# The gates of the banded branch as two column pairs instead of one pair and two single blocks

## The chip, the cores and the metric

The kernel runs on one core of one Trainium2 chip. The metric is the device time of one execution in microseconds (us), as the median of several runs. The profile names the core's engines so: PE is TensorE (matmuls), PEld its weight loads, DVE is VectorE, ACT is ScalarE, POOL is GpSimd and SP is SyncE. SP and POOL here mostly issue DMA transfers.

## The reference

One decoder layer on 256 tokens of width 2048, all in float32. The part that matters here:

```
P  = rms_norm(x) @ W_in            # columns: MLA latents, band q/k/v, gates gA and gB (2048 each)
A  = dense latent attention (16 heads)
Bq = banded attention (32 query heads, 4 kv heads, window 128)
y  = W_out( sigmoid(gA) * (A @ Wo_A) + sigmoid(gB) * (Bq @ Wo_B) )
x  = x + rms_norm(y)
x  = x + rms_norm(conv_ffn(rms_norm(x)))
```

The banded branch's share of the sum is sigmoid(gB) * (Bq @ Wo_B). gB and Bq @ Wo_B are each a product of 256 x 2048 with 2048 x 2048, worked in four blocks of 512 columns.

## The kernel before, in words

**Precision.** Each float32 operand is split into a high part, in the reduced format that TensorE multiplies (`fp32r`), and a low part, the rest. A product is three matmuls: high by high, high by low, low by high (`mm3`, lines 198 to 201). A matmul takes 128 rows of the contraction, 128 tokens and 512 columns.

**Weights.** They stream from HBM in chunks of 128 x 1024 numbers (512 KB). `convert` (lines 153 to 166) lets ACT write the high part `whi` and DVE subtract it to get the low part `wlo`. These go to rings of four slots (`RING`), so an engine can only run four conversions ahead of PE. SP issues the loads into a ring of raw buffers.

**The plain block.** `gemm` (line 203) works 512 columns for both token tiles: 16 row tiles, two to a chunk, 96 matmuls, eight chunks. After each chunk it calls `tick`, which runs the steps that `at(t, f)` has put down for that count of ticks. The program's order is made in this way; a scheduler then orders each engine's queue by readiness and by that order. A queue runs strictly in its order on the chip.

**The pair.** `pair_gemm` (line 274) works 1024 columns, as two halves, for both token tiles, in the manner of Strassen and Winograd: two row tiles, two token tiles and two column halves make a 2 x 2 by 2 x 2 product. Its order string has a letter for each two row tiles. A `p` is a plain unit, two chunks of 12 matmuls each. An `s` is a unit of seven products instead of eight (21 matmuls). Its weights are loaded by POOL's queue (lines 325 to 327) to a place `gr`. DVE makes four sums of them (`weight_sums`, lines 229 to 234), each 128 x 512, into `gta` and `gtb`. Then one conversion each of the odd row tile, half of the even one, `gta` and `gtb`, two ticks in all. For its token side `token_sums` (line 376) makes sums of four 128 x 128 blocks, once for each unit. The pair has four accumulators `c` in one half of PSUM and four `q` in the other; at the end `end_sums` (line 350) adds the `q` into the four tiles `d` and `finish_gate` (line 829) adds `c` and takes the tanh.

**PSUM.** There are eight banks: `pacc` has four, `pss` and `pst` two each. A plain block takes two, from `pacc` unless it is told otherwise; a pair takes all eight, the `q` banks from its first seven-product unit on. `pst` also serves transposes.

**Order around the change.** The last block of latents (line 769, 320 columns) leaves two `pacc` banks that ACT reads (lines 774, 733, 734). Two small transposes of its result (`krT`, `ckT`, lines 779 to 788) follow three and six ticks into the next product. Then come:

1. gate block 0, plain (`gate_b`, line 795);
2. output block 0, Bq @ Wo_B (`out_b`, line 804), with accumulators in `pss`; the token sums of the pair are put down here (line 839);
3. gate blocks 1 and 2 as a pair, order `psppspsp`;
4. output block 1 in `pss`; gate block 3, plain; output block 2 in `pacc`. Over these three run four `park_a` steps (line 843), one in five ticks. Each loads 1 MB of the weights of the last layer part into a buffer `gr`, makes four sums of them on DVE and stores the results in HBM for later (`park_sums`, line 238). There are two `gr` buffers, which the pair's loads use too.

Then comes the dense latent attention, with output block 3 (line 1001) under it. `out_b` ends each block with DVE's product of gate and accumulator (line 807) and a store by POOL's queue (line 808). The gate tiles come from a pool `stg` of four slots.

Of the kernel before, what the change touches and what calls it, by code (L numbers as in the profile page):

```python
# [15 lines left out]
AF = mybir.ActivationFunctionType  # L16
# [3 lines left out]
P = 128  # L20
D = 2048
S = 256
NT = 2
KT = D // P
# [12 lines left out]
C_GB = 5440  # L37
# [5 lines left out]
def trunk_layer(ctx, tc, x, x_cols_in, conv_cols_in, g_mix_post, g_ffn_post, w_in, w_q, w_kv,  # L43
                sinks, rel, wo_a, wo_b, w_out, w_up, w_down, rope_tab, strip_sel, out):
    nc = tc.nc
    vec, act, pe, pool = nc.vector, nc.scalar, nc.tensor, nc.gpsimd
# [7 lines left out]
    pss = ctx.enter_context(tc.tile_pool(name="pss", bufs=2, space=PS))  # L54
# [5 lines left out]
    def sb(pl, shape, name, dt=F32, tag=None, bufs=None):  # L60
        return pl.tile(shape, dt, name=name, tag=tag or name, **({"bufs": bufs} if bufs else {}))
# [41 lines left out]
    cnt = [0]  # L103
# [75 lines left out]
    now = [0]  # L179

    def at(t, *fs):
        steps[max(t, now[0])].extend(fs)
# [10 lines left out]
    def new_acc(tag, ps=None):  # L193
        i = cnt[0]
        pl, pt = ps or (pacc, "acc")
        return [pl.tile([P, 512], F32, name=f"acc{tag}_{i}_{t}", tag=pt) for t in range(NT)]

    def mm3(o, ah, al, bh, bl, start, stop):
        pe.matmul(o, ah, bh, start=start, stop=False)  # L199
        pe.matmul(o, ah, bl, start=False, stop=False)  # L200
        pe.matmul(o, al, bh, start=False, stop=stop)  # L201

    def gemm(xh, xl, w, k0, nk, c0, n, split=None, extra=None, ps=None):

        kc = 1024 // n if n in (256, 512) else 2
        acc = new_acc("g", ps)
        todo = []
        cuts = list(range(0, nk, kc)) + [nk]
        for ci, (k, ke) in enumerate(zip(cuts[:-1], cuts[1:])):
            kk = ke - k  # L210
            src = w[(k0 + k) * P:(k0 + k + kk) * P, c0:c0 + n].rearrange("(a p) n -> p a n", p=P)
            hi, lo = wchunk(src, [kk, n], *(extra or {}).get(ci, ()))
            for j in range(kk):
                kt = k + j
                wh, wl = hi[:, j * n:(j + 1) * n], lo[:, j * n:(j + 1) * n]
                for t in range(NT):
                    x_ = [x(k0 + kt)[:, t * P:(t + 1) * P] for x in (xh, xl)]
                    if split is None or t == 0 or ci < split:
                        mm3(acc[t][:, :n], *x_, wh, wl, kt == 0, kt == (split * kc if split and t else nk) - 1)
                    else:  # L220
                        todo.append((kt, x_, wh, wl))
            tick()
        return acc, todo
# [46 lines left out]
    def park_a(i, pl, tag, t0, **kw):  # L270
        u, p = (i, 0) if i < NA[0] else (i - NA[0], 1)
        return park_sums(f"ta{i}_", w_down, 2 * u, 1024 * p, pl, tag, t0, **kw)
# [186 lines left out]
    XH, XL = pair_view(highs(xt)), pair_view(lows(xt))  # L459
# [6 lines left out]
    rh = sb(base, [P, NT], "rh")  # L466
# [246 lines left out]
    for g in range(4):  # L713
        acc = gemm(XH, XL, w_in, 0, KT, C_QS + 512 * g, 512)[0] if g else acc_q0
# [12 lines left out]
    stg = lambda name, n=512: sb(lpool, [P, n], name, tag="stg", bufs=STG)  # L727
# [36 lines left out]
    acc, _ = gemm(XH, XL, w_in, 0, KT, 0, 512)  # L764
# [4 lines left out]
    acc, _ = gemm(XH, XL, w_in, 0, KT, C_KV, KVR + ROPE)  # L769
# [22 lines left out]
    yb_d = dram.tile([4, NT, P, 512], F32, name="yb_d")  # L792
    x2_d = dram.tile([NT, P, D], F32, name="x2_d")

    def gate_b(j):
        acc, _ = gemm(XH, XL, w_in, 0, KT, C_GB + 512 * j, 512)
        tb = []
        for t in range(NT):
            g = stg(f"tb{j}_{t}")
            act.activation(g, acc[t], AF.Tanh, scale=rh[:, t:t + 1])  # L800
            tb.append(g)
        return tb

    def out_b(j, tb, ps=None):
        acc, _ = gemm(OH, OL, wo_b, 0, KT, 512 * j, 512, ps=ps)
        for t in range(NT):
            vec.scalar_tensor_tensor(tb[t], tb[t], 1.0, acc[t], op0=ALU.add, op1=ALU.mult)
            pool.dma_start(yb_d[j, t], tb[t])
# [4 lines left out]
    esg, pg = open_pool("pg")  # L813
    xs = {}

    def x_sums(u):
        st = sb(pg, [P, 1024], f"xs{u}", F32R)
        a, m = (sb(pg, [P, 512], f"x{n}{u}", tag="x" + n, bufs=1) for n in "am")
        xs[u] = token_sums(xt[u].bitcast(F32), a, m, st[:, 0:512], st[:, 512:1024])
# [2 lines left out]
        both = sb(pg, [P, D], f"gr{cnt[0]}", tag="gr", bufs=2)  # L822
        return both[:, 0:1024], both[:, 1024:2048]

    def gate_pair(j):
        d = [stg(f"tb{j + i}_{t}") for t in range(NT) for i in range(2)]
        c = pair_gemm("g", w_in, 0, C_GB + 512 * j, GATE_ORDER, lambda k, t: (XH(k)[:, t * P:(t + 1) * P], XL(k)[:, t * P:(t + 1) * P]),
                      lambda u: xs[u], 0, d, g_place, lambda: [sb(pg, [P, 1024], f"gt{n}{cnt[0]}", tag="gt" + n, bufs=2) for n in "ab"])
        def finish_gate(i):
            vec.tensor_tensor(d[i], d[i], c[i], op=ALU.add)  # L830
            act.activation(d[i], d[i], AF.Tanh, scale=rh[:, i // 2:i // 2 + 1])

        for n_, i in enumerate((0, 2, 1, 3)):
            at(now[0] + n_, lambda i=i: finish_gate(i))
        return [d[0], d[2]], [d[1], d[3]]

    tb = {0: gate_b(0)}
    for u in range(GATE_ORDER.count("s")):
        at(now[0] + 3 * u, lambda u=u: x_sums(u))
    out_b(0, tb[0], (pss, "s"))  # L840
    tb[1], tb[2] = gate_pair(1)
    parked_b2 = []
    parked_a = [park_a(i, pg, "gr", now[0] + 5 + 5 * i, bufs=2) for i in range(EARLY)]
    out_b(1, tb[1], (pss, "s"))
    tb[3] = gate_b(3)
    out_b(2, tb[2])
    esg.close()


# [148 lines left out]
            q_rope8(u // 4, b + 4 * u)  # L998
        mla_unit(u, b + 4 * u)

    out_b(3, tb[3])
    at_ = [slot("b", p) for p in range(8)]
    ath[:], atl[:] = highs(at_), lows(at_)
    for j in range(4):
        acc, _ = gemm(XH, XL, w_in, 0, KT, C_GA + 512 * j, 512)
        if j == 3:
            both = sb(base, [P, D], "ta3", tag="sg")
        for t in range(NT):
            g = both[:, t * 512:(t + 1) * 512] if j == 3 else stg(f"ta{j}_{t}")
# [106 lines left out]
    for j in range(2, 4):  # L1116
# [4 lines left out]
        acc, _ = gemm(AH, AL, wo_a, 0, KT, 512 * j, 512, ps=(pss, "s") if j == 2 else None)  # L1121
# [82 lines left out]
    for b in range(2, 4):  # L1204
        c0, n = W_BLOCKS[b]
        last = b == 3
        if last:
            flex[0] = "w"
            turn.update(raw=0, w=0)
        acc, todo = gemm(MH_, ML_, w_out, 0, KT, c0, n, split=0 if last else None, extra={i: (px,) for i in range(EXTRA)} if last else None,  # L1210
                         ps=None if last else (pss, "s"))
# [198 lines left out]
    for p in range(2):  # L1410
        d = [dsum[t][2 * p + j] for t in range(NT) for j in range(2)]
        c = pair_gemm(f"d{p}", w_down, 0, 1024 * p, PAIR_ORDER[p], lambda k, t: (GH(k)[:, t * P:(t + 1) * P], GL(k)[:, t * P:(t + 1) * P]),
                      lambda u: s_of[u], p, d, parked=parked_a[NA[0] * p:])
# [109 lines left out]
    def held_into(left):  # L1523
        if left == 6:
            return [sb(base, [P, 1024], f"wh{k}", F32R, tag=f"ahl{k}") for k in (2, 3)]
        if left == 5:
            return [sb(base, [P, 1024], f"wh{k}", F32R, tag=f"ahl{k}") for k in (6, 7)]

    c = pair_gemm("dc", w_down, 24, 1024, B2_ORDER, lambda k, t: (GH(k)[:, t * P:(t + 1) * P], GL(k)[:, t * P:(t + 1) * P]),
                  lambda u: sb_of[u], 1, ud2_tiles, parked=parked_b2, held=held,  # L1530
                  into=held_into)
    for i in range(8):
        unpark(i // 4, i % 4)
    for i in range(4):
        t, j = divmod(i, 2)
# [30 lines left out]
RING = 4  # L1566
A_ORDER = "ppspspsp"
NA_ = A_ORDER.count("s")
GATE_ORDER = "psppspsp"
B_ORDER = "psspsspssp"  # L1570
B2_ORDER = "ppsspssppp"
NB2 = B2_ORDER.count("s")
# [2 lines left out]
EARLY = 4  # L1575
# [76 lines left out]
```

## Time and profile before

| | |
|---|---|
| runs before (3) | median 1458.11 us, 1457.35 to 1458.96 |
| span of the profiled execution | 1453.6 us |
| matmuls | 7522 |
| PE, DVE, ACT, POOL busy | 99%, 80%, 60%, 8% |
| DMA, whole span | 359.74 MB, 247 GB/s |

The span runs from the first instruction to the last of one execution; the time of a run also holds what lies before and after. A busy PE here means that matmuls overlap without a gap, so what a matmul costs is read from the distance between two starts and not from its duration. Rows of the timeline give start, duration, engine, line, operation, output and inputs; the groups by line give count, busy time and mean duration, then the idle time ahead of them and what ended it. Stretches give the busy time of each engine, the granted clock of PE, the DMA engines' share and their rate.

### The profile page before, as it was taken

How to read it: one execution, taken by the hardware profiler on the slowest of the kernel's cores; microseconds unless marked ns; L12 is line 12 of the kernel's file. 1: busy time of each engine (PE TensorE's matmuls, PEld its weight loads, DVE VectorE, ACT ScalarE, POOL GpSimd, SP SyncE). 2: the span in 40 equal slices, each digit the busy share in tenths (PEclk: the TensorE clock that was granted, in tenths of full speed). 3: DMA queues.
4: the chain of work that ended last, by engine and by line, in shares of the span. 5: the costliest groups of instructions: out<-in, count | busy, mean ns of one | idle time of the engine just before them, and what ended most of it. 6: DMA issues, size and time to landing. Idle time of an engine off the chain costs nothing.

```text
span 1453.6 us, 21420 instructions
## 1 busy us (share of the span) xinstructions
PE 1443.9 (99%) x7522; PEld 1233.6 (85%) x7522; DVE 1162.5 (80%) x2034; ACT 866.5 (60%) x1422; POOL 113.6 (8%) x204
## 2 busy tenths in 40 slices
PE   9999999999999999999999999999999999999997
PEld 7888888888898888888888888888888888888886
DVE  7788896766878775888799899876777797986798
ACT  7588864544555655546576565655646565565673
POOL 0012110010000001100000011000000101010000
PEclk9999999999999999999999999999999999999999
DMA  8755376698775759975666898866878888788965
GB/s 301 218 171 163 104 262 193 218 325 292 245 218 175 231 155 321 353 232 177 216 207 212 266 335 302 279 208 213 310 271 268 307 276 291 248 282 275 356 216 208
DMA packets 164744, 359.74 MB, mean 247 GB/s; under 512 B 20843, under 2 KB 32012, under 8 KB 164636
## 3 DMA queue, kind: packets, MB, share of 16 engines
q1 hardware_dynamic: 143296, 282.76, 59.8%
q0 software_dynamic: 21248, 75.56, 15.1%
q8 instruction: 59, 0.97, 0.3%
q14 instruction: 49, 0.40, 0.1%
q10 hardware_dynamic: 92, 0.05, 0.0%
HBM read 323.67 MB, written 34.65 MB: 247 GB/s over the span
## 4 chain that ended last, share of the span: by engine, by line
PE 97%; DVE 1%; ACT 1%; issue 0%; DVEq 0%; ACTq 0%
PE ub L1345 10%; PE ua L1345 10%; PE accg L199 10%; PE accg L201 10%; PE accg L200 10%; PE ub L1349 5%; PE ua L1349 5%; PE cd L200 2%; PE cd L201 2%; PE cd L199 2%; PE cdc L200 1%; PE cdc L199 1%; PE cdc L201 1%; PE mpo L981 1%; PE cdb L200 1%; PE cdb L199 1%
## 5 line engine op out<-in xcount | busy, mean ns | idle before, releaser
L164 ACT CAST whi<-raw 128x1024 fp32r<-128x1024 f32 (+2 forms) x498 | 504.5, 1022 | 374.7 <-PE accg L201 107.6
L165 DVE TENSOR_TENSOR wlo<-raw,whi 128x1024 fp32r<-128x1024 f32 (+2 forms) x498 | 586.1, 1189 | 176.0 <-ACT whi L164 171.4
L199 PE MATMUL accg<-whi,ahl 128*128 128x512 f32 (+1 forms) x416 | 162.8, 391 | 0.0
L201 PE MATMUL accg<-whi,ahl 128*128 128x512 f32 (+1 forms) x416 | 160.7, 386 | 0.0
L200 PE MATMUL accg<-wlo,ahl 128*128 128x512 f32 (+1 forms) x416 | 159.9, 384 | 0.0
L1345 PE MATMUL ub<-ahl,whi 128*128 128x512 f32 x640 | 154.7, 391 | 0.0
L1345 PE MATMUL ua<-ahl,whi 128*128 128x512 f32 x640 | 154.6, 391 | 0.0
L1345 PEld LDWEIGHTS ub<-ahl,whi 128*128 128x128 f32 x640 | 117.5, 188 | 22.8 <-ACT cc L1237 0.2
L1345 PEld LDWEIGHTS ua<-ahl,whi 128*128 128x128 f32 x640 | 117.5, 188 | 22.7
L199 PE MATMUL accg<-whi,bhl 128*128 128x512 f32 x256 | 100.7, 393 | 0.0
L201 PE MATMUL accg<-whi,bhl 128*128 128x512 f32 x256 | 99.9, 390 | 0.0
L200 PE MATMUL accg<-wlo,bhl 128*128 128x512 f32 x256 | 99.8, 390 | 0.0
L201 PEld LDWEIGHTS accg<-whi,ahl 128*128 128x128 f32 x416 | 78.1, 188 | 15.5
L200 PEld LDWEIGHTS accg<-wlo,ahl 128*128 128x128 f32 x416 | 78.2, 188 | 13.2
L199 PEld LDWEIGHTS accg<-whi,ahl 128*128 128x128 f32 x416 | 78.2, 188 | 12.9
L1349 PEld LDWEIGHTS ub<-ahl,wlo 128*128 128x128 f32 x640 | 82.3, 191 | 3.2
L1349 PEld LDWEIGHTS ua<-ahl,wlo 128*128 128x128 f32 x640 | 82.2, 191 | 3.1
L1349 PE MATMUL ua<-ahl,wlo 128*128 128x256 f32 x640 | 83.7, 283 | 0.0
L1349 PE MATMUL ub<-ahl,wlo 128*128 128x256 f32 x640 | 83.3, 283 | 0.0
L201 PEld LDWEIGHTS accg<-whi,bhl 128*128 128x128 f32 x256 | 48.0, 188 | 10.1
L200 PEld LDWEIGHTS accg<-wlo,bhl 128*128 128x128 f32 x256 | 48.1, 188 | 9.7
L199 PEld LDWEIGHTS accg<-whi,bhl 128*128 128x128 f32 x256 | 48.1, 188 | 9.6
(660 smaller groups left out, 2682.7 us busy)
## 6 DMA issues: line engine op xcount, KB each, us to landing
raw<-in_ffn_w_up_dram SPq DMA_DIRECT2D x142, 512.0 KB, 4.8
raw<-in_w_in_dram SPq DMA_DIRECT2D x105, 512.0 KB, 4.6
raw<-in_ffn_w_down_dram SPq DMA_DIRECT2D x66, 512.0 KB, 5.7
xraw<-in_ffn_w_up_dram SPq DMA_DIRECT2D x34, 512.0 KB, 5.1
raw<-in_w_o_swa_dram SPq DMA_DIRECT2D x32, 512.0 KB, 4.8
raw<-in_w_o_mla_dram SPq DMA_DIRECT2D x26, 512.0 KB, 5.9
raw<-in_w_out_dram SPq DMA_DIRECT2D x26, 512.0 KB, 4.6
ta_s<-in_ffn_w_down_dram POOLq DMA_DIRECT2D x24, 512.0 KB, 6.2
```

Source lines behind the costliest of these rows:

```text
L164: act.copy(hi[:, a:b], raw[:, a:b])
L165: vec.tensor_tensor(lo[:, a:b], raw[:, a:b], hi[:, a:b].bitcast(F32), op=ALU.subtract)
L199: pe.matmul(o, ah, bh, start=start, stop=False)
L200: pe.matmul(o, ah, bl, start=False, stop=False)
L201: pe.matmul(o, al, bh, start=False, stop=stop)
L981: pe.matmul(o, w(t), p_[:, c], start=n == 0, stop=n == 5)
L1345: pe.matmul(acc[i], hi[:, c], hn[p][:, j * 512:(j + 1) * 512], start=p + j == 0, stop=stop)
L1349: pe.matmul(acc[i][:, 0:256], lo[:, c], hn[p][:, j * 512:j * 512 + 256], start=False, stop=False)
```

## The change

All four gate blocks are worked as two pairs, blocks 0 and 1 with order `pppspssp` and blocks 2 and 3 with `psppspsp`. The first pair stands where gate block 0 stood. Output blocks 0 and 1 follow, then the second pair, then output block 2. With that move:

- the token sums are put down ahead of the first pair, at ticks 0, 3 and 7;
- the four parked sums run over output blocks 0 and 1, one in three ticks instead of five;
- output block 1 takes its accumulators from `pacc` and output block 2 from `pss`;
- a pair's four gate tiles are taken from `stg` when its sums end, and no longer at its start; `out_b` asks for them after its product.

```diff
-    def gate_b(j):
-        acc, _ = gemm(XH, XL, w_in, 0, KT, C_GB + 512 * j, 512)
-        tb = []
-        for t in range(NT):
-            g = stg(f"tb{j}_{t}")
-            act.activation(g, acc[t], AF.Tanh, scale=rh[:, t:t + 1])
-            tb.append(g)
-        return tb
-
-    def out_b(j, tb, ps=None):
+    def out_b(j, tb_of, ps=None):
         acc, _ = gemm(OH, OL, wo_b, 0, KT, 512 * j, 512, ps=ps)
+        tb = tb_of()
         for t in range(NT):
             vec.scalar_tensor_tensor(tb[t], tb[t], 1.0, acc[t], op0=ALU.add, op1=ALU.mult)
             pool.dma_start(yb_d[j, t], tb[t])
...
-    def gate_pair(j):
-        d = [stg(f"tb{j + i}_{t}") for t in range(NT) for i in range(2)]
-        c = pair_gemm("g", w_in, 0, C_GB + 512 * j, GATE_ORDER, lambda k, t: (XH(k)[:, t * P:(t + 1) * P], XL(k)[:, t * P:(t + 1) * P]),
-                      lambda u: xs[u], 0, d, g_place, lambda: [sb(pg, [P, 1024], f"gt{n}{cnt[0]}", tag="gt" + n, bufs=2) for n in "ab"])
+    def gate_pair(j, order):
+        d = []
+
+        def gate_tiles():
+            d[:] = [stg(f"tb{j + i}_{t}") for t in range(NT) for i in range(2)]
+            return d
+
+        c = pair_gemm(f"g{j}", w_in, 0, C_GB + 512 * j, order, lambda k, t: (XH(k)[:, t * P:(t + 1) * P], XL(k)[:, t * P:(t + 1) * P]),
+                      lambda u: xs[u], 0, gate_tiles, g_place, lambda: [sb(pg, [P, 1024], f"gt{n}{cnt[0]}", tag="gt" + n, bufs=2) for n in "ab"])
...
-        return [d[0], d[2]], [d[1], d[3]]
-
-    tb = {0: gate_b(0)}
-    for u in range(GATE_ORDER.count("s")):
-        at(now[0] + 3 * u, lambda u=u: x_sums(u))
-    out_b(0, tb[0], (pss, "s"))
-    tb[1], tb[2] = gate_pair(1)
+        return lambda i: (d[i], d[2 + i])
+
+    for u in range(GATE_ORDER[0].count("s")):
+        at(now[0] + (0, 3, 7)[u], lambda u=u: x_sums(u))
+    tb = gate_pair(0, GATE_ORDER[0])
     parked_b2 = []
-    parked_a = [park_a(i, pg, "gr", now[0] + 5 + 5 * i, bufs=2) for i in range(EARLY)]
-    out_b(1, tb[1], (pss, "s"))
-    tb[3] = gate_b(3)
-    out_b(2, tb[2])
+    parked_a = [park_a(i, pg, "gr", now[0] + 5 + 3 * i, bufs=2) for i in range(EARLY)]
+    for j in range(2):
+        out_b(j, lambda j=j: tb(j), None if j else (pss, "s"))
+    tb = gate_pair(2, GATE_ORDER[1])
+    out_b(2, lambda: tb(0), (pss, "s"))
     esg.close()
...
-    out_b(3, tb[3])
+    out_b(3, lambda: tb(1))
...
-GATE_ORDER = "psppspsp"
+GATE_ORDER = ("pppspssp", "psppspsp")
```

## The prediction, made before the result

> **What bounds the kernel now.** I read the profile from the whole to the stage. First the page: span, busy time, chain of waits.
>
> ```profile
> span 1453.6 us, 21420 instructions
> ...
> PE 1443.9 (99%) x7522; PEld 1233.6 (85%) x7522; DVE 1162.5 (80%) x2034; ACT 866.5 (60%) x1422; POOL 113.6 (8%) x204
> ...
> PE 97%; DVE 1%; ACT 1%; issue 0%; DVEq 0%; ACTq 0%
> ```
>
> PE is busy 99% of the span and is 97% of the chain that ended last. So fewer matmuls are worth their full time, as long as nothing makes PE wait. The median of the runs, 1458.11 us, is 4.5 us above this execution's span of 1453.6 us. What lies around the span is the same in both kernels, so I work out a difference against the span and add it to the median. A measurement of this kernel can tell about 0.2%, 2.9 us, from no change.
>
> Next, the view of stretches, cut at the stages of the banded branch: gate block 0, output block 0, the gate pair, output block 1, gate block 3, output block 2.
>
> ```profile
> core 0: us, PE busy (x) PEld busy (x) DVE busy (x) ACT busy (x) POOL busy (x), PEclk, DMA share, GB/s
> 196.00:218.60 22.60, 22.60 (x105) 18.68 (x105) 22.10 (x58) 13.25 (x25) 2.97 (x5) 1.00 0.85 290
> 218.60:240.40 21.80, 21.80 (x98) 18.06 (x97) 13.45 (x15) 9.87 (x11) 0.00 (x0) 1.00 0.69 209
> 240.40:282.20 41.80, 41.80 (x184) 34.33 (x183) 29.27 (x32) 21.91 (x23) 4.27 (x8) 1.00 0.59 200
> 282.20:304.00 21.80, 21.80 (x98) 18.05 (x97) 15.68 (x18) 10.91 (x12) 2.14 (x4) 1.00 0.83 272
> 304.00:325.80 21.80, 21.80 (x98) 18.06 (x97) 15.93 (x18) 8.77 (x9) 4.31 (x8) 1.00 0.96 333
> 325.80:347.50 21.70, 21.70 (x98) 17.96 (x97) 12.38 (x13) 9.36 (x10) 1.07 (x2) 1.00 0.97 310
> ```
>
> PE is full in all six, at a granted clock of 1.00. Two other columns matter. DVE is full in the first stretch (22.10 of 22.60 us) and loose afterwards. The DMA engines are nearly full in the last two (0.96 and 0.97).
>
> **What a matmul costs.** The timeline of PE gives the first matmul of each stage; the groups by line give the pair's count.
>
> ```profile
> 196.28 0.39 PE L199 MATMUL accg<-whi,ahl 128*128 128x512 f32 x1
> ...
> 218.82 0.39 PE L199 MATMUL accg<-whi,bhl 128*128 128x512 f32 x1
> ...
> 240.58 0.39 PE L199 MATMUL cg<-whi,ahl 128*128 128x512 f32 x1
> ...
> 282.43 0.39 PE L199 MATMUL accg<-whi,bhl 128*128 128x512 f32 x1
> ```
> ```profile
> L199 PE MATMUL cg<-whi,ahl 128*128 128x512 f32 x46 | 17.9, 390 | 0.0
> ...
> L199 PE MATMUL qg<-whi,xs 128*128 128x512 f32 x9 | 3.5, 393 | 0.0
> L199 PE MATMUL cg<-whi,xs 128*128 128x512 f32 x3 | 1.2, 404 | 0.0
> ...
> L199 PE MATMUL qg<-whi,ahl 128*128 128x512 f32 x3 | 1.2, 389 | 0.0
> ```
>
> A 512-column block is 16 row tiles x 2 token tiles x 3 = 96 matmuls. Output block 0 takes 240.58 - 218.82 = 21.76 us, so one more matmul costs 0.227 us; the 0.39 us of a row is its latency, which overlaps the next. The Trainium skill (TensorE: Matmul & The Clock Gate, "Back-to-back issue gap") gives about 131 ns for such a matmul in a stream; by that, nine would be an estimated 1.2 us. The sum goes by the trace's 0.227 us.
>
> The pair is (46 + 9 + 3 + 3) x 3 lines = 183 matmuls, as its order says: five plain units of 24 and three seven-product units of 21. It takes 282.43 - 240.58 = 41.85 us, 0.36 us more than 183 x 0.227.
>
> **Removed and added on PE.** Removed: gate blocks 0 and 3. Block 0 takes 218.82 - 196.28 = 22.54 us, of which 22.54 - 21.76 = 0.78 us are the transposes of the latent and the rotary key, which stay. Block 3 is another 21.76 us. Added: one pair, 41.85 us. The difference is 41.85 - 2 x 21.76 = -1.67 us: nine matmuls (2.04 us) less the 0.36 us. This is all there is to win, 0.11%. ACT's tanh count stays; each block gains one addition per token tile, on a DVE that is loose by then.
>
> **DVE in the first pair.** The pair now starts at 196.28, in the stretch where DVE is full, and everything that once lay a stage ahead of it (token sums, the weight sums of two units) must fit inside it. Prices are start-to-start distances:
>
> ```profile
> 217.13 0.29 DVE L382 TENSOR_TENSOR xm<-xa 128x128 f32<-128x128 f32 x1
> 217.34 0.29 DVE L383 TENSOR_TENSOR xm<-xm,xa 128x128 f32<-128x128 f32 x1
> ...
> 220.51 0.69 DVE L232 TENSOR_TENSOR gta<-gr 128x512 f32<-128x512 f32 x1
> 221.11 0.69 DVE L233 TENSOR_TENSOR gtb<-gr,gta 128x512 f32<-128x512 f32 x1
> 221.71 1.22 DVE L165 TENSOR_TENSOR wlo<-raw,whi 128x1024 fp32r<-128x1024 f32 x1
> 222.84 0.69 DVE L234 TENSOR_TENSOR gtb<-gr,gtb 128x512 f32<-128x512 f32 x1
> ```
> ```profile
> L165 DVE TENSOR_TENSOR wlo<-raw,whi 128x1024 fp32r<-128x1024 f32 x8 | 9.7, 1218 | 0.0
> L378 DVE TENSOR_TENSOR xa<-ahl 128x512 f32<-128x512 f32 x3 | 2.1, 684 | 0.0
> L418 DVE TENSOR_TENSOR xs<-xm,xs 128x512 fp32r<-128x512 f32 x2 | 1.4, 686 | 0.0
> L231 DVE TENSOR_TENSOR gta<-gr 128x512 f32<-128x512 f32 x2 | 1.4, 682 | 0.0
> ```
>
> 128 wide: 0.2 us. 512 wide: 0.6. A low half of 1024: 1.13. So a seven-product unit costs DVE four sums (2.4) and low halves of 1024 three times and of 512 once (3.99): 6.4 us, against 21 x 0.227 = 4.76 us of PE. A token sum is 0.6 + 4 x 0.2 + 0.6 = 2.0 us, three are 6.0. The old first stretch held 8 low halves (9.0), three first and two last steps of token sums (3.0), their twelve narrow steps (2.4) and five weight sums (two of line 231, one of each of the next three lines; 3.0): 17.4 of 22.10 us. The other 4.7 us are the latent's and key's steps, which stay.
>
> Before PE can do the last unit's second half, DVE needs 4.7 + 6.0 + 3 x 6.4 + six plain low halves (8 less two that were ready at the start) 6.8 = 36.7 us, so it is there at 232.7. PE gets there after 8 x 12 + 42 + 15 = 153 matmuls and the transposes: 196.28 + 34.7 + 0.8 = 231.8. DVE is late by about 0.9 us if it never idles; nothing if some of the latent's steps slip behind it.
>
> **Banks.** The pair takes four accumulators at once where block 0 took two, and four more at its first seven-product unit.
>
> ```profile
> 197.97 0.41 ACT L734 ACTIVATE accg<-ck 128x256 f32<-128x256 f32 x1
> ...
> 198.68 0.22 ACT L734 ACTIVATION_READ_ACCUMULATOR accg<-ck 128x1 f32 x1
> ```
> ```profile
> 217.57 0.48 DVE L421 SCALAR_TENSOR_TENSOR ckl<-ckT,gmat,ckh 128x256 fp32r<-128x256 f32 x1
> ...
> 303.90 1.28 DVE L807 SCALAR_TENSOR_TENSOR tb<-tb,accg 128x512 f32<-128x512 f32 x2
> ```
>
> Two of the first four still hold the latent block: ACT is done with them at about 198.4 and 198.9, while PE wants them six and nine matmuls in, at 197.6 and 198.3: up to 0.8 us, with the rest of PE's queue behind it, nothing if the next row tile's products for free banks come first. The last of the second four is the transposed latent's, read until 218.05; PE wants it 72 + 15 matmuls and the transposes in, at 216.8: up to 1.2 us. These do not add to DVE's lateness, since a PE that lost time early meets DVE's deadlines later. Together: 0 to 2 us, below nothing impossible for a wait; I take **1.1 us**, the middle, since the two bank rows and DVE's 0.9 all lie near it. At the other seam, output block 1 moves into two of the second pair's four banks: its two products (1.28 us, begun as PE ends) free them before PE's sixth and ninth matmul (1.36 and 2.04 us). I cost it at nothing; a conversion ahead of them on DVE would make it up to 1.1 us.
>
> **POOL and DMA.** The parked sums move from three stages to output blocks 0 and 1, one per three chunks (12 matmuls, 2.72 us) instead of five; their loads, stores and the second pair's loads share two buffers and POOL's queue.
>
> ```profile
> 294.77 0.54 POOL L263 DMA_DIRECT2D ta<-ta_s  x1 [2.17 <-DVE ta_s L253]
> ...
> 300.59 1.06 POOL L246 DMA_DIRECT2D ta_s<-in_ffn_w_down_dram  x2 [5.28 <-DMA ta<-ta_s]
> ```
> ```profile
> raw<-in_w_o_swa_dram SPq DMA_DIRECT2D x32, 512.0 KB, 4.8
> ...
> ta_s<-in_ffn_w_down_dram POOLq DMA_DIRECT2D x24, 512.0 KB, 6.2
> ta<-ta_s POOLq DMA_DIRECT2D x24, 512.0 KB, 5.2
> ...
> gr<-in_w_in_dram POOLq DMA_DIRECT2D x6, 512.0 KB, 5.1
> ```
>
> POOL stands until a store has landed, 5.8 us after its issue, and a load takes 6.2: 12 of the 13.6 us from one sum's second half to the same buffer's next sum (five chunks). Queued behind POOL's wait are yb_d stores, which nobody needs soon; behind a late sum on DVE are low halves, of which four ring slots keep PE supplied for two chunks. The second pair's first load can go 5.8 us after the third sum's second store (chunk 12 of 16), some 5 us before that pair, whose first seven-product unit comes after 24 matmuls (5.4 us). Cost: nothing.
>
> **Sum:** -1.67 + 1.1 = -0.6 us: span 1453.0, median **1457.5 us**.
>
> **Rivals.** *All of it hidden*: the waits are filled, and the full 1.67 us shows: 1456.4. For it: in the trace weight sums and token sums run far ahead of their place (gta at 220.51, for a pair that begins at 240.58). Against: DVE has no room left at 196 to 219.
>
> *DVE sets the first pair's pace* (slower). If the weight sums are not spread ahead of their units, each unit is 6.4 us of DVE against 4.76 of PE: three times 1.66 = 5.0 us, less 1.67: +3.3, 1461.4. It decides once DVE enters the first unit with no sums done. For it: the 22.10 of 22.60. Against: six plain row tiles come first in this order.
>
> *The DMA engines fill up*. Output blocks 0 and 1 would move 16 weight chunks, eight stores, four loads of parked sums, and two gate loads at 0.524 MB, and 0.5 MB of results: 16.2 MB in 43.5 us. The stretch with 333 GB/s at share 0.96 allows 347 GB/s: 46.8 us, 3.3 late, less 1.67: 1459.7. Against: the last store and the gate loads (2.1 MB) can land later, and the rest fits. The Trainium skill (SBUF — State Buffer, "A bandwidth-pool intuition that's wrong (but worth ruling out)") puts the path from HBM to a core at about 358 GB/s; by that the same bytes would take an estimated 45.3 us. No stretch here exceeds it.
>
> That the change does not remove nine matmuls is excluded by the counts above.
>
> **How the numbers follow.** Forecast 0.56, all hidden 0.22, DMA 0.11, DVE's pace 0.11. The full gain is 1.67 us, so a gain over 2.9 us needs something not seen here: 0.04, from the second case. Slower by over 2.9 us is DVE's case and a little of DMA's: 0.12. The rest, 0.84, is within 0.2%. The range runs from the full gain with the 0.36 us of the pair saved too (1456.1) to above DMA's case: 1456.0 to 1460.2; outside lie DVE's case and small parts of the others.
>
> **What would show it.** PE with nine matmuls fewer (7513, some records may be missing); two pairs of 41.9 to 44 us; the first one longer, its waits at the third and fourth accumulator, at the sixth of its second banks and at the low half of the last unit's sums; DVE full from 196 to about 235; output blocks at 21.8 us. I am wrong if the first pair takes over 46 us, if output blocks 0 and 1 stretch with the DMA share near 1, or if the stages after the branch change by more than 1 us.

## The result and the profile after

The changed kernel takes 1474.03 us (median of five runs, 1472.19 to 1477.55); the kernel before took 1457.48 us beside it (five runs). The ratio is 1.0114, 95% interval 1.0097 to 1.0131: 1.1% slower, where no change was forecast. The execution profiled after took 1472.34 us, 1470.5 of it span. Lines of `out_b` and below have numbers 3 to 8 lower than before: the product of gate and accumulator is L799, its store L800.

The page of the changed kernel, busy times and chain:

```profile
PE 1449.0 (99%) x7513; PEld 1234.2 (84%) x7513; DVE 1179.5 (80%) x2060; ACT 871.4 (59%) x1429; POOL 117.0 (8%) x210
...
PE 51%; DVE 3%; DMA 2%; issue 1%; ACT 0%; DVEq 0%; ACTq 0%
```

The nine matmuls are gone (7513 against 7522). The chain is no guide here. Its shares add up to 57%, against 99% before, because it is followed back only to a transfer at 638 us and no further; the banded branch lies ahead of that, so nothing in this line is about the change. Where the time went, the view of stretches tells, cut at the first pair, output blocks 0 and 1, the second pair, and output block 2. The last three columns are the granted clock, the DMA engines' share and GB/s.

```profile
197.00:241.00 44.00, 43.48 (x192) 34.79 (x192) 43.45 (x85) 27.04 (x40) 6.12 (x11) 1.00 0.66 229
241.00:262.80 21.80, 21.80 (x98) 18.06 (x97) 18.83 (x22) 10.93 (x12) 3.20 (x6) 1.00 0.86 291
262.80:286.30 23.50, 22.02 (x98) 17.91 (x97) 11.60 (x14) 7.39 (x7) 4.54 (x9) 1.00 0.91 330
286.30:342.00 55.70, 46.37 (x185) 36.52 (x184) 38.55 (x44) 22.84 (x24) 4.05 (x8) 0.88 0.56 186
342.00:364.00 22.00, 22.00 (x99) 18.22 (x98) 13.28 (x14) 10.90 (x12) 0.00 (x0) 1.00 0.78 226
```

Output block 1 is longer by 1.7 us, and the second pair takes 55.7 where the pair before took 41.8. It is also the only stretch with a clock under 1.00. The timeline of PE has the first matmul of each stage and those that had to wait (in brackets the idle time of the engine ahead of the instruction, and what ended it):

```profile
197.27 0.39 PE L199 MATMUL cg<-whi,ahl 128*128 128x512 f32 x1
...
218.83 0.47 PE L199 MATMUL qg<-whi,xs 128*128 128x512 f32 x1 [0.24 <-DVE ckl L421]
...
233.34 0.50 PE L199 MATMUL qg<-whi,xs 128*128 128x512 f32 x1 [0.23 <-ACT whi L164]
...
241.22 0.39 PE L199 MATMUL accg<-whi,bhl 128*128 128x512 f32 x1
...
262.98 0.39 PE L199 MATMUL accg<-whi,bhl 128*128 128x512 f32 x1
...
283.89 0.50 PE L200 MATMUL accg<-wlo,bhl 128*128 128x512 f32 x1 [1.48 <-DVE wlo L165]
...
286.51 0.39 PE L199 MATMUL cg<-whi,ahl 128*128 128x512 f32 x1
293.84 0.80 PE L200 MATMUL cg<-wlo,ahl 128*128 128x512 f32 x1 [6.94 <-DVE wlo L165]
294.43 0.63 PE L201 MATMUL cg<-whi,ahl 128*128 128x512 f32 x1
294.86 0.63 PE L199 MATMUL cg<-whi,ahl 128*128 128x512 f32 x1
...
298.63 0.79 PE L199 MATMUL cg<-whi,ahl 128*128 128x512 f32 x1 [2.29 <-DVE tb L799]
...
342.17 0.39 PE L199 MATMUL accg<-whi,bhl 128*128 128x512 f32 x1
```

From start to start: first pair 43.95 us, output block 0 21.76, output block 1 23.53, second pair 55.66; together 144.90. Before, the same work took 86.15 + 2 x 21.76 = 129.67. So 15.2 of the 16.9 us of span lie here, 13.8 of them in the second pair. The branch also begins 0.99 us later (197.27 against 196.28), after stages that the change doesn't touch; some 0.7 us come behind it. The later start differs from kernel to kernel here (the first pair's first weight load lies between 195.82 and 197.65 us in kernels with the same work ahead of it), so I don't count it as the change's.

PE waits three times for DVE: for low halves at 283.89 and at 293.84, and at 298.63 for output block 1's product, which holds a bank. What DVE waits for, its own timeline says:

```profile
272.43 1.23 DVE L165 TENSOR_TENSOR wlo<-raw,whi 128x1024 fp32r<-128x1024 f32 x1 [0.79 <-ACT whi L164]
278.69 0.69 DVE L253 TENSOR_TENSOR ta_s<-ta_s 128x512 f32<-128x512 f32 x1 [5.04 <-DMA ta_s<-in_ffn_w_down_dram]
282.01 0.69 DVE L253 TENSOR_TENSOR ta_s<-ta_s 128x512 f32<-128x512 f32 x1 [2.62 <-DMA ta_s<-in_ffn_w_down_dram]
282.62 1.22 DVE L165 TENSOR_TENSOR wlo<-raw,whi 128x1024 fp32r<-128x1024 f32 x1
...
291.36 0.69 DVE L231 TENSOR_TENSOR gta<-gr 128x512 f32<-128x512 f32 x1 [6.92 <-DMA gr<-in_w_in_dram]
...
292.57 1.22 DVE L165 TENSOR_TENSOR wlo<-raw,whi 128x1024 fp32r<-128x1024 f32 x1
```

DVE stands for a parked sum's load, and then for the load of the second pair's first weight sum, `gta`, which the scheduler put ahead of the low half at 292.57. That low half is ready at 293.79, and PE goes on at 293.84. And the loads are late because POOL, which issues them, stands for stores:

```profile
258.94 1.06 POOL L246 DMA_DIRECT2D ta_s<-in_ffn_w_down_dram  x2 [4.43 <-DMA ta<-ta_s]
...
271.60 1.07 POOL L246 DMA_DIRECT2D ta_s<-in_ffn_w_down_dram  x2 [6.79 <-DMA ta<-ta_s]
...
273.19 0.54 POOL L263 DMA_DIRECT2D ta<-ta_s  x1
284.98 0.54 POOL L326 DMA_DIRECT2D gr<-in_w_in_dram  x1 [11.26 <-DMA ta<-ta_s]
```

The second pair's first load goes out at 284.98, 11.8 us after the third sum's second store at 273.19, for whose landing POOL stood 11.26 us. The view of DMA issues from 240 to 300 us has the medians from issue to landing (last column):

```profile
ta<-ta_s POOLq DMA_DIRECT2D x8, 512.0 KB, 8.7
...
ta_s<-in_ffn_w_down_dram POOLq DMA_DIRECT2D x4, 512.0 KB, 7.4
```

A parked sum's store and the next load into its buffer take 8.7 + 7.4 = 16.1 us, where 13.6 were there. The clock, last: from 290.20, inside the longest wait, the stretch to 303.80 has

```profile
290.20:303.80 13.60, 7.67 (x17) 5.61 (x18) 9.08 (x12) 2.61 (x3) 3.78 (x7) 0.50 0.82 280
```

At a granted clock of 0.50 matmuls start 0.43 us apart (294.43 to 294.86) instead of 0.227. For some 15 of them that is 3.0 us; the waits in output block 1 and the second pair are about 13.0 us, summed over the distances between weight loads in excess of 0.227.

### The profile page after: what moved, and what is told of

Its sections match the earlier page's. It is cut to its first block, busy times and chain, and to the rows that moved or that the text cites. A ratio compares the mean times of both kernels' runs of the same rounds, so it can differ in the third digit from the quotient of the medians.

```text
span 1470.5 us, 21440 instructions
## 1 busy us (share of the span) xinstructions
PE 1449.0 (99%) x7513; PEld 1234.2 (84%) x7513; DVE 1179.5 (80%) x2060; ACT 871.4 (59%) x1429; POOL 117.0 (8%) x210
## 2 busy tenths in 40 slices
DMA packets 162696, 359.74 MB, mean 245 GB/s; under 512 B 20843, under 2 KB 32012, under 8 KB 162588
## 4 chain that ended last, share of the span: by engine, by line
PE 51%; DVE 3%; DMA 2%; issue 1%; ACT 0%; DVEq 0%; ACTq 0%
PE ua L1341 10%; PE ub L1341 10%; PE ub L1345 5%; PE ua L1345 5%; PE cd L200 2%; PE cd L199 2%; PE cd L201 2%; PE accg L199 2%; PE accg L201 2%; PE accg L200 2%; DVE wlo L165 1%; DMA raw<-in_ffn_w_down_dram 1%; DMA mr1hi<-in_w_out_dram 1%; PE cw L199 1%; PE qd L200 1%
## 5 line engine op out<-in xcount | busy, mean ns | idle before, releaser
L164 ACT CAST whi<-raw 128x1024 fp32r<-128x1024 f32 (+2 forms) x492 | 498.3, 1022 | 361.0 <-PE accg L201 101.5
L165 DVE TENSOR_TENSOR wlo<-raw,whi 128x1024 fp32r<-128x1024 f32 (+2 forms) x492 | 578.4, 1187 | 161.3 <-ACT whi L164 152.9
L199 PE MATMUL accg<-whi,ahl 128*128 128x512 f32 (+1 forms) x352 | 137.7, 391 | 0.0
L201 PE MATMUL accg<-whi,ahl 128*128 128x512 f32 (+1 forms) x352 | 135.7, 385 | 0.0
L200 PE MATMUL accg<-wlo,ahl 128*128 128x512 f32 (+1 forms) x352 | 134.9, 383 | 0.0
L201 PEld LDWEIGHTS accg<-whi,ahl 128*128 128x128 f32 x352 | 66.1, 188 | 12.9
L200 PEld LDWEIGHTS accg<-wlo,ahl 128*128 128x128 f32 x352 | 66.2, 188 | 10.7
L199 PEld LDWEIGHTS accg<-whi,ahl 128*128 128x128 f32 x352 | 66.2, 188 | 10.4
```

Source lines behind the costliest of these rows:

```text
L164: act.copy(hi[:, a:b], raw[:, a:b])
L165: vec.tensor_tensor(lo[:, a:b], raw[:, a:b], hi[:, a:b].bitcast(F32), op=ALU.subtract)
```

## Experiments

Three theories stood against each other. **A**: a chain. The parked sums and the pair's loads take turns in two buffers and in one queue, each load waits for a store, and DVE, in its fixed order, passes the lateness on to PE. **B**: the bytes alone fill the DMA engines. **C**: the second pair is slow by itself, in its new place. Ratios are to the kernel before, run on the same chip (median 1456.1 to 1456.9 us).

### The spacing alone

`x1_before_park3`, on the kernel before:

```diff
-    parked_a = [park_a(i, pg, "gr", now[0] + 5 + 5 * i, bufs=2) for i in range(EARLY)]
+    parked_a = [park_a(i, pg, "gr", now[0] + 5 + 3 * i, bufs=2) for i in range(EARLY)]
```

> The kernel before with its four parked sums three ticks apart instead of five, nothing else. Theory A (in the changed kernel a parked load lands late because it must wait for an earlier store to free one of two buffers, DVE stands at that sum with low halves queued behind it, then the next pair's own loads wait for the same buffers, PE idles and its clock halves): here no pair follows, so DVE stands a few us at the third or fourth sum, PE loses 0 to 2 us, the clock stays at 1: 1457.5 to 1460. Theory B (the bytes in output blocks are too many for the DMA engines, whatever the buffers): as many bytes in as little time, so a loss of 5 us or more: over 1462. Theory C (the second pair itself is slow where it stands): no change, 1457.5.

Measured: 1461.0 us (1457.17 to 1462.19), ratio 1.0026 [1.0009, 1.0043]. One wait of PE, 3.3 us, in gate block 3, and DVE ahead of it in the same stance as above:

```profile
324.18 0.69 DVE L253 TENSOR_TENSOR ta_s<-ta_s 128x512 f32<-128x512 f32 x1 [7.83 <-DMA ta_s<-in_ffn_w_down_dram]
```

Three chunks apart, the parked sums stall a kernel that has no second pair. But they cost it 0.26%, not 1.1%. The time lies between what A (to 1460) and B (over 1462) had expected, and against A the granted clock did fall, to 0.50 for 3.4 us.

`x2_park5` is the changed kernel with the five chunks of before (the same line, the other way).

> The changed kernel with the parked sums five ticks apart again, so that the last two fall at the end of output block 1 and into the second pair. Theory A: each buffer has time for its store and the next load, but the last two parked sums hold the pair's buffers; most of the 16.5 us comes back: 1457 to 1464, clock near 0.998. Theory B: fewer bytes per us, all of it comes back: 1456 to 1458. Theory C: 1472 to 1475 as before.

Measured: 1470.51 us, 1.0104 [1.0087, 1.012]. The output blocks are clean, at a higher DMA share than in the changed kernel, and the whole loss sits in the second pair: its first seven-product unit waits 8.8 us (by the list of PE's waits) for one late load. None of the three theories had this time. In the stretches of output blocks 0 and 1, and in POOL's timeline:

```profile
240.25:262.00 21.75, 21.75 (x97) 18.02 (x96) 16.15 (x18) 10.92 (x12) 2.13 (x4) 1.00 0.84 292
262.00:283.80 21.80, 21.80 (x98) 18.06 (x97) 15.03 (x19) 7.39 (x7) 4.30 (x8) 1.00 0.96 329
```
```profile
279.96 0.54 POOL L263 DMA_DIRECT2D ta<-ta_s  x1 [1.91 <-DVE ta_s L253]
290.11 0.53 POOL L326 DMA_DIRECT2D gr<-in_w_in_dram  x1 [9.61 <-issue]
```

The pair's load goes out 10.15 us after a store, 6 us into the pair. What ended POOL's 9.61 us ahead of it the profile doesn't name; that it was the store is argued from the other kernels. So the spacing is not enough of a cause: what was a stall of output block 1 becomes one of the pair.

### Is it the second pair itself?

`x4_first_only` keeps the first pair, and makes blocks 2 and 3 plain blocks again, with parked sums five chunks apart:

```diff
-    tb = gate_pair(2, GATE_ORDER[1])
+    tb = gate_b(2)
     out_b(2, lambda: tb(0), (pss, "s"))
+    tb = gate_b(3)
```

> The first half of the change alone: blocks 0 and 1 as the first pair, blocks 2 and 3 plain, parked sums five ticks apart over output block 0, output block 1 and gate block 2. As many matmuls as before (375 for the gates). All theories: the first pair costs what it cost in the changed kernel, some 1.2 us of PE waiting at its banks, so 1458 to 1459.5 against 1457.5; theory C would put the whole loss into the other half, as A does, so this run only says whether the first pair is harmless.

Measured: 1458.59 us (ten runs), 1.0015 [1.0006, 1.0024]. The first pair shows its three small waits and the rest is clean. Against `x2_park5` (1.0104), which has the same spacing, the loss needs the second pair.

`x6_early0` keeps both pairs and puts the four early parked sums with the other eight, later in the kernel (`EARLY = 0`, and one in 6 ticks there instead of 7.5).

> The changed kernel without parked sums in the banded branch: all twelve are made in the later part (every six ticks there instead of every seven and a half). Theories A and B: both output blocks and the second pair run at PE's pace; what is left is the gain of 1.67 us less some 1.2 us at the first pair's banks, and whatever the denser parked sums cost later: 1455.5 to 1458. Theory C (the second pair itself): over 1465.

Measured: 1462.19 us (1460.1 to 1467.81, ten runs), 1.0036 [1.0019, 1.0053]. The stretches of the first pair, the two output blocks and the second pair:

```profile
196.92:240.82 43.90, 43.35 (x192) 34.67 (x190) 43.27 (x85) 27.02 (x40) 6.13 (x11) 1.00 0.65 225
240.82:262.60 21.78, 21.78 (x98) 18.04 (x97) 18.40 (x22) 11.03 (x12) 0.00 (x0) 1.00 0.72 240
262.60:284.34 21.74, 21.74 (x98) 18.00 (x96) 10.98 (x11) 8.44 (x8) 1.10 (x2) 1.00 0.71 221
284.34:326.20 41.86, 41.86 (x185) 34.31 (x183) 29.33 (x33) 21.91 (x23) 2.16 (x4) 1.00 0.45 148
```

The second pair takes 41.86 us, as the pair before did: C is out. The four stretches add up to 129.28 us, 0.39 less than before. The total is above what A and B expected (to 1458): time is lost later, where the parked sums now stand closer and PE waits for low halves.

### Bytes, or the order in which they wait?

`x8_half`: the early parked sums load and store half of their columns, in the same order on DVE and POOL; the last layer part reads plain weights in their place, so its output isn't the layer's.

```diff
-                ins = pool.dma_start(st[0][:, i * 1024:(i + 1) * 1024], w[(k + i) * P:(k + i + 1) * P, c0:c0 + 1024])
+                n = 512 if tag == "gr" else 1024
+                ins = pool.dma_start(st[0][:, i * 1024:i * 1024 + n], w[(k + i) * P:(k + i + 1) * P, c0:c0 + n])
...
-            pool.dma_start(td[0], st[0][:, 0:1024])
+            pool.dma_start(td[0][:, 0:n], st[0][:, 0:n])
```

> The changed kernel with the four early parked sums loading and storing half the columns (256 KB a transfer instead of 512), DVE and POOL in the same order with as many instructions of the same size; the sums are then taken of the loaded half alone and the last part reads plain weights in their place, so its output isn't the layer's. Theory A (the chain of waits over two buffers, at any rate): transfers keep most of their time, the waits stay: 1465 or more. Theory B (bytes): transfers land in time, DVE does not stand, PE keeps its clock: 1456 to 1460.

Measured: 1465.1 us, 1.0055 [1.0037, 1.0073]. Both hold a part. With half the bytes the output blocks are clean. The pair still waits twice, and POOL still stands for a store ahead of the pair's load, at 278.21:

```profile
278.21 0.54 POOL L333 DMA_DIRECT2D gr<-in_w_in_dram  x1 [8.01 <-DMA ta<-ta_s]
```

`x3_gr3` gives the shared place a third buffer (`bufs=3` at both uses).

> The changed kernel with three buffers instead of two for the parked sums and the pairs' loads; spacing three ticks as in the change. Theory A: the fourth parked load and the second pair's first load no longer wait for a store; DVE does not stand at them, PE keeps its clock: 1456 to 1461. Theory B: the same bytes in the same time, loads late all the same: 1468 or more. Theory C: 1472 to 1475.

Measured: 1467.66 us, 1.0086 [1.0069, 1.0103], far over A's 1461 and just under B's 1468. A third buffer moves the wait and shortens it, but the load stands behind a store's landing as before, and DVE behind the load:

```profile
273.62 0.54 POOL L326 DMA_DIRECT2D gr<-in_w_in_dram  x1 [9.29 <-DMA ta<-ta_s]
```
```profile
278.46 0.69 DVE L231 TENSOR_TENSOR gta<-gr 128x512 f32<-128x512 f32 x1 [10.12 <-DMA gr<-in_w_in_dram]
```

`x12_share_wide` has eight chunks between parked sums in the two shared buffers (`5 + 8 * i`).

> The changed kernel with the parked sums one in eight chunks instead of three, in the two shared buffers as before. It parts the two things that the kernel with an own buffer changed at once: the spacing and the buffer. The second pair's loads are still issued behind parked stores, since they take turns in the two buffers. Theory A with the buffers as the cause: at least one wait of 2 us or more stays in the second pair's first half, at a unit whose load was issued behind a wait for a store, and the time is 1459 to 1466. Theory A with the spacing alone as the cause, as the kernel before with its five chunks ran clean: no wait over 1 us, and 1455.5 to 1458.5, as with the own buffer. Theory B (bytes): the parked traffic per us is less than half of the changed kernel's, so it expects no wait either.

Measured: 1464.34 us, 1.0049 [1.0034, 1.0064]; PE waits 4.5 us at the second pair's seventh matmul, with one load issued ahead of the pair but behind a store. Even this far apart the pair's loads wait for parked stores, as theory A with the buffers as the cause had it. The spacing matters too: from three chunks to eight, in the same buffers, the time falls from 1.0114 to 1.0049, some 9.5 us.

### DVE's order

`x5_keep` holds the second pair's weight sums in program order on DVE, so that no low half of an earlier chunk stands behind them:

```diff
+        kept = tc.keep_in_program_order if name == "g2" else lambda ins: ins
-        vec.tensor_tensor(ta[:, a], even[:, b], even[:, a], op=ALU.subtract)
+        kept(vec.tensor_tensor(ta[:, a], even[:, b], even[:, a], op=ALU.subtract))
```

> The changed kernel with the second pair's weight sums kept in the program's order on DVE, so that they no longer stand ahead of the low halves of output block 1 and of the pair's first plain unit. Theory A (late parked loads; two buffers; DVE's queue in order): the parked sums are as late as before, so PE still loses some 2 us in output block 1; the 7.5 us wait inside the pair's first plain unit goes, in its place PE waits at the first seven-product unit for its late load, perhaps 3 to 6 us: 1462 to 1469. Theory B (bytes alone): no change, 1470 or more.

Measured: 1471.58 us, 1.0096 [1.0071, 1.0121]. That is B's range and not A's. The wait for a low half in the first plain unit is gone, but one of 9.3 us stands five matmuls later in the same unit, at the bank that output block 1 holds: DVE's product, which frees it, now stands behind a low half of the late weights, for which ACT waited 16.5 us. So it didn't move to the first seven-product unit, as A had it. The order on DVE decides where PE stops, and hardly for how long.

`x7_park_split` leaves one parked sum in each output block, five chunks apart, and moves two to the second pair's last unit and output block 2 (`5 + (0, 5, 25, 28)[i]`).

> The changed kernel with two parked sums five ticks apart over output blocks 0 and 1 and two over output block 2, none near the second pair. Theory A: the second pair's first load finds its buffer free; no long wait: 1455.5 to 1459. Theory B: fewer bytes in output blocks 0 and 1, but the same rate in output block 2, so a loss there of a few us: 1458 to 1464.

Measured: 1467.25 us (1462.92 to 1469.36), 1.0063 [1.0045, 1.0081]. Both theories had expected less (to 1459 and to 1464). Half the parked sums out of the way is no cure: DVE still stands 5.73 and 8.18 us for the pair's loads, which wait their turn in the same buffers.

### The pair's loads out of the chain

`x9_own` lets the pairs keep the two buffers, and gives the early parked sums one of their own:

```diff
-    parked_a = [park_a(i, pg, "gr", now[0] + 5 + 3 * i, bufs=2) for i in range(EARLY)]
+    parked_a = [park_a(i, pg, "gp", now[0] + 5 + 8 * i) for i in range(EARLY)]
```

> The changed kernel, but the pairs keep the two shared buffers for themselves, and the four early parked sums get one buffer of their own, one sum in eight chunks (over the two output blocks and the second pair). So the loads for the second pair's first two units are issued by POOL ahead of any wait for a parked store. Nothing is left out, no byte more or fewer is moved. Theory A (the pair's loads stand behind stores and parked sums in shared buffers, and DVE behind them): no wait over 1 us in the output blocks and the second pair, that pair 41.9 to 42.6 us at a clock of 1.00, time 1455.5 to 1457.5 us, at or below the kernel before. Theory B (bytes alone fill the DMA engines): the same bytes in the output blocks less one parked sum; a wait of 2 us or more stays, over 1460. The third theory, that the second pair is slow by itself: over 1465.

Measured: 1457.47 us (1455.22 to 1458.77, eleven runs), 1.0008 [0.9999, 1.0017]. POOL issues the second pair's first two loads at 226 and 232 us, while the first pair still runs, instead of 285 and 297. The stretches:

```profile
196.90:240.87 43.97, 43.33 (x192) 34.66 (x191) 43.35 (x85) 27.00 (x40) 7.16 (x13) 1.00 0.70 247
240.87:262.60 21.73, 21.73 (x97) 18.01 (x96) 20.57 (x26) 10.84 (x12) 2.13 (x4) 1.00 0.81 286
262.60:284.40 21.80, 21.80 (x98) 18.03 (x97) 13.63 (x16) 8.44 (x8) 3.23 (x6) 1.00 0.95 333
284.40:326.50 42.10, 42.10 (x184) 34.20 (x183) 32.06 (x38) 21.90 (x23) 5.38 (x10) 1.00 0.62 222
```

All the change's work, the same 359.74 MB over the kernel, and output block 1 at 333 GB/s and share 0.95 without a wait. That takes back the 1.1%, and speaks against B as the cause. Against `x12_share_wide`, with the same eight chunks (1.0049), some 6 us come from the buffers alone. The own buffer is also a third one; that a third shared one would not do as well was tried only at three chunks (`x3_gr3`, 1.0086). The time lies at the upper edge of what A expected, and it isn't below the kernel before: the four stretches sum to 129.60, against 129.67.

`x10_own_wide` has nine chunks, the first sum one chunk later (`6 + 9 * i`).

> As the kernel with one own buffer for the parked sums, but one sum in nine chunks, the first one chunk later; the last one ends in output block 2 or under the last chunks of the pair. Theory A: the same as with eight chunks within 1 us, since the spacing no longer touches the pair's loads: 1455.5 to 1457.5. If the spacing still matters (the own buffer's reload waits for its store, and a late load holds DVE), this one has shorter waits than the one at eight chunks; over 1460 in both would speak against A.

Measured: 1459.09 us, 1.0021 [1.0012, 1.0029], 1.6 over what was expected. PE waits once, 2.8 us, for a low half behind a weight sum. The third load of the second pair is again behind a parked store in POOL's queue:

```profile
285.52 0.54 POOL L246 DMA_DIRECT2D ta_s<-in_ffn_w_down_dram  x1 [4.88 <-DMA ta<-ta_s]
...
287.65 0.54 POOL L326 DMA_DIRECT2D gr<-in_w_in_dram  x1
```

In `x9_own` that load stood behind such a wait as well; it went out at 286.49 and cost PE nothing. Here it went 1.2 us later, and the sum that reads it started 4.1 us later (295.76 against 291.66). So an own buffer doesn't take away every risk: a load that stays queued behind the wait for a store can still be late.

### The clock, and the second seam

`x11_warm` puts 120 small matmuls ahead of the second pair, to keep PE busy while the load is late:

```diff
+        if name == "g2":
+            for i in range(120):
+                tc.keep_in_program_order(pe.matmul(c22[:, 0:P], ramp, ramp, start=True, stop=True))
```

> The changed kernel with 120 matmuls of 128 columns on a constant, into the fourth accumulator, directly ahead of the second pair: PE works where it would else stand for the late load. It adds work that the result doesn't use. It separates two parts of the loss there, the wait itself (about 10 us of the second pair's 13.8) and the matmuls at half the granted clock after it (about 3.0 us). If the halved clock follows from PE standing still: the waits inside the pair shrink by about what the added matmuls take (7 us or so), the clock in the pair is at 1.00 for all but a few us, and the time falls by 1 to 3 us against the changed kernel: 1471 to 1473. If the clock is halved for another reason (the load of the DMA engines or of all engines together), the half-rate stretch stays at about 13 us, and the time doesn't fall: 1474 or more.

Measured: 1475.76 us, 1.0127 [1.0111, 1.0143]. The expectation failed: waits of 11.6 us stayed (by the weight loads, as the 13.0 above), one of them in output block 1, where the added matmuls can't reach, and 2.8 us of half rate. It settles the order of things, though. Stretches after the first wait (4.3 us, ending at 287.2), between, and after the second (4.1 us, ending at 303.4):

```profile
287.00:290.00 3.00, 2.85 (x7) 2.28 (x8) 0.70 (x2) 0.00 (x0) 1.58 (x3) 0.50 0.60 175
290.00:303.70 13.70, 9.32 (x130) 8.18 (x129) 7.55 (x10) 1.57 (x2) 1.67 (x4) 1.00 0.71 209
303.70:307.10 3.40, 3.40 (x9) 2.62 (x8) 1.12 (x3) 0.00 (x0) 2.10 (x4) 0.50 1.02 340
```

The clock halves behind each long wait, at a DMA share of 0.60 as at 1.02, and not between. Whether filling the whole wait would save the 3.0 us was not shown.

`x13_seam` moves output block 1's accumulators out of the second pair's first four banks, with every engine's order unchanged. They lie in two of its `q` banks instead, which the pair takes only at its first seven-product unit, 24 matmuls in; so it is not quite true that no bank of the pair holds them:

```diff
-        out_b(j, lambda j=j: tb(j), None if j else (pss, "s"))
+        out_b(j, lambda j=j: tb(j), (pst, "t") if j else (pss, "s"))
```

> The changed kernel, but output block 1 takes its two accumulators from the banks that otherwise serve transposes, so no bank of the second pair holds it; each engine's instructions stand in the same order. If the seam is a cause of its own, the wait of 3.35 us at the second pair's accumulators goes without replacement, with its share of the half-rate matmuls: 1469 to 1471.5. If the seam is only where PE first meets the late load, the wait for low halves or for the first seven-product unit grows by what the seam gives up: 1472.5 to 1475, waits of 12 to 13.5 us in the output blocks and the second pair as before.

Measured: 1475.03 us (1472.76 to 1479.69), 1.0126 [1.0105, 1.0147], no gain, and waits of 15.2 us by the weight loads, more than either theory had; but the traced execution took 1479.69 us, 4.7 over the median. The waits of PE (total, times, longest):

```profile
PE cg L200 <- DVE wlo L165: 5.9, 1, 5.9
PE accg L200 <- DVE wlo L165: 4.2, 1, 4.2
PE qg L200 <- DVE wlo L165: 3.8, 1, 3.8
```

The wait at the bank is gone, and one of 3.8 us for low halves has come at the seven-product unit. The seam is only one of the places where PE meets the late loads.

## Why the prediction was wrong

**Nine matmuls, -1.67 us: right.** 7513 matmuls; undisturbed, the second pair takes 41.86 us (`x6_early0`), against 41.85 of the sum.

**First pair's waits, +1.1 us: right in place, a little short.** 43.95 less 41.85 and 0.78 is 1.32 us. The q bank of the transposed latent ends one wait (218.83, DVE L421), and the idle time ahead of the pair's weight loads is put down to ACT's reading of the latent block for 0.5 us:

```profile
L199 PEld LDWEIGHTS cg<-whi,ahl 128*128 128x128 f32 x92 | 18.1, 197 | 7.3 <-DVE tb L799 3.0 <-ACT accg L734 0.5
```

The last unit's wait (233.34) ends with ACT's high part, where the prediction had DVE's low half. DVE is full, as foreseen, at 43.45 of 44.00 us. In `x6_early0` these terms add up to -0.39 us against the forecast's -0.6, so that part of the sum held.

**Second seam, nothing: right as a cause.** Its bank waits came from the late load (`x13_seam`).

**"POOL and DMA", "Cost: nothing": this step failed.** It is 13.0 us of waits and 3.0 us of half-rate matmuls. Four things in it went wrong:

- The durations. It used 5.8 us for a store and 6.2 for a load, from the trace of before, where sums were five chunks apart: 12 of 13.6 us, 1.6 to spare. From 240 to 300 us of the changed kernel they are 8.7 and 7.4 at the median, 16.1 together. The store's 5.8 us were one row, from output block 1 (share 0.83). In the next stage before, at share 0.96, stood a slower one:

```profile
310.32 0.54 POOL L263 DMA_DIRECT2D ta<-ta_s  x1 [1.97 <-DVE ta_s L253]
317.81 1.06 POOL L246 DMA_DIRECT2D ta_s<-in_ffn_w_down_dram  x2 [6.95 <-DMA ta<-ta_s]
```

The load went out 7.5 us after the store. With 6.8, the median of the parked loads between 282 and 348 us, that makes 14.3, over the 13.6 already. The medians of that stretch, 6.0 and 6.8, would still have fitted. A sum over budget here is late for all that follows, since POOL issues nothing behind the store that it waits for.
- The pair's own load. It was to go 5.8 us after the third sum's second store, and went 11.8 us after it, 1.5 us before the pair. The rest of its argument, 24 matmuls of grace to the first seven-product unit, was lost on DVE: the sum stands ahead of low halves that PE needs sooner.
- The cover. The prediction took four ring slots as two chunks, 5.4 us. The trace gives more: DVE ended a low half at 273.66 and began the next at 282.62, and PE ran on until the matmul at 282.02, about 8.4 us. But DVE stood 5.04 and 2.62 us, with two sums between, and that used it up; the 6.92 us that follow reach PE almost whole, as 6.94.
- The price of a wait on PE. None was set for the clock.

The Trainium skill (DMA: Bandwidth & Descriptors, "Anatomy of one DMA — SWDGE (gpsimd) path") says that a wait on a semaphore is made by the issuing sequencer, ahead of the dispatch; POOL's rows show it, with 11.26 us. Its fit there, about 2 us and the bytes at 436 GB/s, would make 512 KB an estimated 3.2 us; the stores here took 8.7 at the median, and the measurement decides.

**The rival of full DMA engines** named the place and the sign (1459.7), not the mechanism: `x9_own` moves the same work at share 0.95 and 333 GB/s with no stall. The bytes have a part in it: in `x8_half` the parked stores, of 256 KB, take 5.8 us at the median from 240 to 300 us instead of 8.7, its output blocks are clean, and the ratio falls from 1.0114 to 1.0055. But with the same bytes, and the pair's first loads queued ahead of the parked stores, the loss is gone.

**The forecast's own warning** held: output block 1 stretched with the share at 0.91. With the pair's first loads ahead of the stores (`x9_own`) the loss is gone, but the gain of the sum isn't shown either: 1.0008 [0.9999, 1.0017] lies just above its -0.6 us (0.9996), and the four stages take 129.60 us against 129.67.

## What to carry to other kernels

When transfers move to a fuller stage, take their durations from the slowest rows of the fullest stage in the trace, not from one row or the median, and add store and reload of each buffer against the spacing: with 1.6 of 13.6 us to spare, assume that it breaks. Then ask of each late load what stands behind it, first in the queue that issues it and then on the engine that reads it. Give loads with a due time buffers that no store holds, and queue them ahead of every wait for a store.

## What the runs showed of the hardware

- **The clock after a wait.** A wait of 2.8 us (`x10_own_wide`) left the granted clock at 1.00; after one of 3.3 us (`x1_before_park3`) it was 0.50 for 3.4 us; after 6.94 us here, with 2.29 more in the stretch, for 13.6. The Trainium skill (TensorE: Matmul & The Clock Gate, "Why this matters for your kernels") warns of idle gaps over about 3 us on PE, and these three agree. But in `x5_keep` a wait of only 2.5 us (PE idle until 284.10) was followed by 0.50 from 285.4, for 3.4 us. So here the length of a wait alone doesn't decide, and 3 us is no safe limit. The length at half clock, by the traces' clock records, came in pieces of about 3.4 us (3.4 in `x1_before_park3`, 6.8 in `x8_half`, 10.2 in `x2_park5`, 13.6 here).
- **Stores under load.** The same 512 KB store took 5.2 us at the median of the whole span before, 6.0 in its fullest stretch (282 to 348 us), and 8.7 in the changed kernel from 240 to 300 us; at the worst row above, 11.8 us passed from a store's issue to the next load's. With the own buffer (`x9_own`) the median from 240 to 300 us was 5.5 us, for five stores instead of eight, at a share of 0.81 and 0.95 in the two output blocks. So the share alone doesn't set it; what else does was not tried.
